# Hybrid diffusion step on one core: row sums beside the out-projection, a last part of three tiles with the prompt tile turned alone, and the first weight sums on VectorE

## The chip, the cores and the metric

The kernel runs on one core of one Trainium2 chip. The metric is the device time of one execution in microseconds (us). The core has five engines with queues of their own: PE (TensorE; its weight loads are listed as PEld), DVE (VectorE), ACT (ScalarE), POOL (GpSimd) and SP (SyncE, which here only issues DMAs). They run side by side and wait for each other by semaphores; each executes its own queue in order. SBUF holds tiles of 128 partitions; PE writes to PSUM.

## What is computed

One layer of a diffusion backbone for 128 prompt tokens and 1024 sample tokens (a 64 x 16 grid), width 1024, float32. Cut to what matters:

```python
def trunk_layer(x, mod, ...):
    shift1, scale1, gate1, shift2, scale2, gate2 = jnp.split(mod, 6, axis=-1)
    h = rmsnorm(x, norm1) * (1 + scale1) + shift1
    mix, new_gla, new_hgrn = hybrid_mixer(h, ...)      # ends with  merged @ w_out
    x = x + gate1 * mix
    h = rmsnorm(x, norm2) * (1 + scale2) + shift2
    x = x + gate2 * conv_ffn(h, w_ffn_up, ffn_conv, b_ffn_conv, w_ffn_down, grid)
    return x, new_gla, new_hgrn

def conv_ffn(h, w_up, conv_w, conv_b, w_down, grid):
    u = dw_conv(h @ w_up, conv_w, conv_b, grid)        # 3x3 over the grid, width 3 for the prompt
    gate, up = jnp.split(u, 2, axis=-1)                # 2816 hidden columns each
    return (jax.nn.silu(gate) * up) @ w_down
```

Both kinds of token go through `trunk_layer` with their own modulation; a last rmsnorm gives `y_prompt` and `y_sample`. The states of the mixer are outputs too and lie ahead of what is changed.

## The kernel before

**Split products.** All large products are made from two parts of each operand: a high part (fp32r, made by ACT as a copy, names ending in `h`) and a low part, the operand less its high part (`split_lo`, line 69, a subtraction on DVE or POOL, names ending in `l`). Each product is three matmuls: high x high, high x low, low x high. So every operand of a product costs one ACT operation and one DVE or POOL operation after it is there.

**Stages.** The mixer runs to about 722 us. Then comes the out-projection `merged @ w_out` with the residual sum, the second norm and its modulation; then the up projection with convolution and gating in 22 chunks of 128 hidden columns (2 x 128 columns of `w_ffn_up` a chunk); then the down projection. The change touches the handover from the mixer to the up projection.

**Out-projection (loop `g` over three groups of three token tiles; lines 1379 and 1392).** Tiles 0 to 7 are sample tokens, tile 8 is the prompt. For groups 0 and 1 most of the product was made beside the mixer and stored; only head block 7 is left. For group 2 (tiles 6, 7, 8) all eight blocks `f` of `w_out` are multiplied here, in the order 1, 2, 0, 3, 4, then 5, 6, 7 tile by tile as the last part, so that the three tiles end one after the other. For each finished tile, `done(i)` multiplies by `gate1` (DVE, L1365), adds x (DVE, L1366) into a tile `x1`, stores it to DRAM (POOL's queue, L1367), makes the reciprocal root of the mean square (`rstd_of`: a Square with a row sum on ACT L377, which writes its squares to `junk`; a small DVE operation L378; a power on POOL L379), and scales into `xn` (ACT, L1370).

**Turning (`modulate2`, line 1314).** PE turns `xn` in 128 x 128 blocks (`transpose`), so that width lies on partitions. For each of eight width blocks `kt` the three tiles of a group go into one PSUM tile; ACT (L1327, odd `kt`) and DVE (L1331, even `kt`) scale and shift it into `RAW[i, j]` (tiles `rb`: i = half of the width, j = half of the sample tokens) and, for tile 8, into `raw_p`.

**Up projection (line 1499).** The sample tokens' product of a chunk is made from seven products of half size in place of eight, in the manner of Strassen: the token operands are b11, b21, b22 and the sums t1 to t4 of `rb` tiles; the weight operands are the four blocks 11, 12, 21, 22 of the chunk and the sums s1 to s4. For a chunk: `load_row` (L1470, SP) loads blocks into `ra`; `weight_sums` (L1490 to 1493, POOL) makes s1 to s4 in `sr`; `split_slots` (ACT L1485, POOL L69) splits into nine slots of the weight tiles `W`. A plan (`plan_slots`) gives the slots of each chunk. The token sums and their splits are made once, on DVE with ACT for the high parts, between lines 1530 and 1562: t1, the prompt (`ph`, `pl`), t2, b22, t3, t4. `queued` writes this order out by hand: each step is put behind the one before on DVE, and on ACT too where it has an ACT part. The sums lie in `tmp[0..3]`, which are the accumulators `acc0..3` of the convolution, not in use yet. The order of the products of the first chunk on PE is 1 (b11), 2 (b21), 5 (t1), prompt, 6 (t2), 3 (b22), prompt, 7 (t3), then the second chunk's 5, then 4 (t4). The prompt's product (L1704) is 12 matmuls in each of two halves, over two weight slots at a time.

**Convolution and gating.** `conv_rows` makes the grid's convolution of a half chunk as one ACT operation (L1628) and eight DVE operations (L1640) that read PSUM. Then Silu (ACT, L1734), the product of the two halves (POOL, L1736), and the store to DRAM (`scr_g`, L1737); `token_sums` makes sums of two chunks for the down projection (POOL, L1593 to 1597).

**Down projection (line 1910).** Again products of half size, 11 pairs of chunks each. Operands are loaded from `scr_g`, `scr_s` and `w_ffn_down` (L128) into raw buffers that are used in turn: quarters of `ra` and `sr`, and two tiles `raw0`, `raw1` of a pool `wh3` on the right side of SBUF, which is opened when the pools of the up projection are closed. ACT makes the high part (L131), DVE or POOL the low part (L69). The pools share SBUF: a tile of a later pool waits until the last reader of the tile that lay there is done.

**What sets the order.** The order of each engine's queue is decided when the program is built, by the framework's planner, which puts operations by estimated times; `issue_after` and `queued` put constraints on it by hand (so do `anchor`'s entries). `next_w` and `prefetch_w` hand out the split weights of the mixer's and the down projection's streams, with loads some slots ahead.

## Time and profile before

| | |
|---|---|
| median of 3 runs | 1573.55 us (1572.3 to 1575.32) |
| the profiled execution | 1575.3 us, of which 1573.2 is the span of the instructions |
| mean granted TensorE clock in it | 0.983 |
| busy: PE, PEld | 1500.9 us (95%), 1258.8 us (80%) |
| busy: DVE, ACT, POOL | 1153.2 us (73%), 788.5 us (50%), 726.3 us (46%) |
| up projection L1499 in the chain that ended last | 26% |
| DMA | 244.61 MB, 155 GB/s mean |

All times within the profile count from the start of the span. A row of the timeline is: start, duration, engine, line, operation, output <- inputs, shape, and how often; in brackets the idle time of the engine just before it and what ended that. "x2" rows cover two instructions from the first start on. A row of the waits is: engine, line and tile that waited <- what released it: us in total, times, longest. A row of the chain of waits is: start, duration, what; it follows the work that ended last back from the end, so that each piece is released by the one above it. A row of the DMA issues gives the median us from issue to landing.

### The profile page before, as it was taken

What the parts mean: (1) busy time and instruction counts of PE and PEld (TensorE: products, weight loads), DVE (VectorE), ACT (ScalarE), POOL (GpSimd) and SP (SyncE); (2) the same over time, 40 slices, a digit from 0 to 9 for tenths busy, and PEclk for the clock granted to TensorE, in tenths of its full rate; (3) what the DMA queues carried; (4) which work ended last, traced back from release to release, by engine and by line L of the source; (5) the groups of instructions that cost most, each with busy time, mean ns of one, the idle gap of its engine ahead of it and who ended that gap; (6) DMA issues with size and microseconds to landing.
All of it is one profiled execution on the core that took longest, in us unless ns stands there. A gap on an engine that the chain in (4) does not pass through costs nothing.

```text
span 1573.2 us, 31068 instructions
## 1 busy us (share of the span) xinstructions
PE 1500.9 (95%) x12506; PEld 1258.8 (80%) x12506; DVE 1153.2 (73%) x1724; ACT 788.5 (50%) x1521; POOL 726.3 (46%) x535
## 2 busy tenths in 40 slices
PE   7999999999999999898879999999999998999997
PEld 2698989998898989676657888888888886788886
DVE  3656566565655768535689999999999999579575
ACT  3565667455454556304564444444444444456444
POOL 1412132234232331102288999999999996000001
PEclk9999999999999999999979999999999999999999
DMA  9311112336434452747411555545644566879762
GB/s 341 113 44 46 46 53 76 96 105 214 113 129 159 133 168 95 297 157 273 158 41 56 169 171 138 131 117 135 197 117 135 176 160 192 321 243 348 248 190 116
DMA packets 164650, 244.61 MB, mean 155 GB/s; under 512 B 11124, under 2 KB 107618, under 8 KB 162586
## 3 DMA queue, kind: packets, MB, share of 16 engines
q1 hardware_dynamic: 142583, 168.54, 33.4%
q0 software_dynamic: 21312, 73.41, 15.2%
q8 instruction: 98, 1.61, 0.4%
q10 hardware_dynamic: 611, 0.68, 0.1%
q14 instruction: 46, 0.38, 0.1%
HBM read 186.95 MB, written 78.71 MB: 169 GB/s over the span
## 4 chain that ended last, share of the span: by engine, by line
PE 82%; DVE 6%; DMA 5%; ACT 3%; issue 3%; POOL 2%; SPq 0%; POOLq 0%; ACTq 0%; DVEq 0%
PE u L1499 26%; PE mm L602 15%; PE xb L1910 7%; PE yb L1910 6%; PE mm L616 5%; PE x L1704 4%; PE mm L745 4%; PE lv L933 3%; PE yb L1961 2%; PE u L1392 2%; PE x L1001 1%; PE mm L505 1%; DMA raw<-in_w_in_dram 1%; DMA wa<-in_w_ada_dram 1%; PE ada L1170 1%
## 5 line engine op out<-in xcount | busy, mean ns | idle before, releaser
L1640 DVE SCALAR_TENSOR_TENSOR acc<-u,convc,acc 128x945 f32<-128x945 f32 (+2 forms) x352 | 427.0, 1218 | 8.3 <-ACT acc L1628 1.7
L69 POOL TENSOR_TENSOR wl<-raw,wh 128x1024 fp32r<-128x1024 f32 x42 | 102.0, 2432 | 247.3 <-ACT wh L131 189.7
L602 PE MATMUL mm<-h1h,wh 128*128 128x384 f32 x528 | 184.9, 350 | 0.7 <-ACT qj L514 0.7
L602 PE MATMUL mm<-h1h,wl 128*128 128x384 f32 x528 | 179.1, 339 | 0.0
L602 PE MATMUL mm<-h1l,wh 128*128 128x384 f32 x528 | 179.1, 339 | 0.0
L896 DVE TENSOR_TENSOR Q<-Q,fb 128x384 f32<-128x384 f32 x126 | 85.9, 682 | 92.6 <-PE lv L933 91.3
L69 POOL TENSOR_TENSOR wul<-sr,wuh 128x512 fp32r<-128x512 f32 (+1 forms) x68 | 123.7, 1820 | 25.8 <-ACT wuh L1485 25.6
L69 POOL TENSOR_TENSOR wul<-ra,wuh 128x1024 fp32r<-128x1024 f32 x46 | 118.9, 2585 | 9.2 <-ACT wuh L1485 6.1
L886 ACT ACTIVATE m<-k 128x384 f32<-128x384 f32 x126 | 70.2, 557 | 83.7 <-DVE k L898 39.4
L1885 POOL TENSOR_TENSOR sq<-sq,mhalf 128x1 f32<-128x1 f32 x9 | 11.1, 1237 | 216.7 <-DVE sq L1882 216.7
L602 PEld LDWEIGHTS mm<-h1h,wh 128*128 128x128 f32 x528 | 99.5, 188 | 5.6 <-issue 3.9
L602 PEld LDWEIGHTS mm<-h1l,wh 128*128 128x128 f32 x528 | 99.5, 188 | 0.6 <-issue 0.2
L602 PEld LDWEIGHTS mm<-h1h,wl 128*128 128x128 f32 x528 | 99.3, 188 | 0.8 <-issue 0.5
L616 PE MATMUL mm<-wh,h1h 128*128 128x256 f32 x288 | 84.4, 293 | 1.3 <-ACT v L641 1.3
L898 DVE TENSOR_TENSOR k<-k,fb 128x384 f32<-128x384 f32 x126 | 74.2, 589 | 12.3 <-ACT m L886 7.2
L131 ACT ACTIVATE wh<-raw 128x1024 fp32r<-128x1024 f32 x55 | 58.2, 1059 | 48.8 <-PE mm L602 11.6
L616 PE MATMUL mm<-wh,h1l 128*128 128x256 f32 x288 | 80.9, 281 | 0.0
L616 PE MATMUL mm<-wl,h1h 128*128 128x256 f32 x288 | 80.9, 281 | 0.0
L1485 ACT ACTIVATE wuh<-ra 128x1024 fp32r<-128x1024 f32 x44 | 46.3, 1053 | 38.0 <-issue 36.1
L1669 ACT ACTIVATE u2p<-u 128x512 f32<-128x512 f32 x44 | 26.3, 597 | 74.4 <-PE u L1499 71.7
L1485 ACT ACTIVATE wuh<-sr 128x512 fp32r<-128x512 f32 (+1 forms) x66 | 50.9, 773 | 22.9 <-PE x L1704 17.0
L1736 POOL TENSOR_TENSOR acc<-acc,acc 128x1152 f32<-128x1152 f32 x22 | 59.1, 2687 | 5.8 <-DVE acc L1640 5.8
(355 smaller groups left out, 4518.6 us busy)
## 6 DMA issues: line engine op xcount, KB each, us to landing
ra<-in_w_ffn_up_dram SPq DMA_DIRECT2D x88, 256.0 KB, 3.1
raw<-in_w_in_dram SPq DMA_DIRECT2D x32, 512.0 KB, 4.6
v<-in_w_ada_dram SPq DMA_DIRECT2D x27, 512.0 KB, 4.4
scr_g<-acc POOLq DMA_DIRECT2D x22, 576.0 KB, 5.5
scr_s<-late POOLq DMA_DIRECT2D x11, 1024.0 KB, 4.6
scr_t<-in_w_ffn_down_dram POOLq DMA_DIRECT2D x16, 704.0 KB, 7.4
wa<-in_w_ada_dram SPq DMA_DIRECT2D x16, 512.0 KB, 6.2
raw<-in_w_out_dram SPq DMA_DIRECT2D x13, 512.0 KB, 3.8
```

The source lines that it names most:

```text
L69: return eng.tensor_tensor(out, full, hi.bitcast(F32), op=ALU.subtract)
L602: anchor["fill"] = mm(ps, a[:, kt, :], h[kt][b], start=(n == 0), stop=(n == 23))
L616: anchor["fill"] = mm(ps, h[kt][t // 3][:, ts_], a[:, kt % 4, :], start=(n == 0), stop=(n == 23))
L745: anchor["fill"] = mm(ps, lhs, ws[f][wi][:, cs], start=(f + n == 0), stop=(f == 6 and n == 2))
L886: nc.scalar.activation(aps(t, 0, [[2 * h, NB], [h, 2], [1, h]]), aps(src, 0, [[2 * h, NB], [BL + h, 2], [1, h]]), AF.Copy)
L896: nc.vector.tensor_tensor(qm, qm, aps(ff_, 2 * h - 1, [[BL - h, 2], [2 * h, NB], [0, h]]), op=ALU.mult)
L898: nc.vector.tensor_tensor(km, km, aps(ff_, BL + 2 * h - 1, [[-(BL + h), 2], [2 * h, NB], [0, h]]), op=ALU.mult)
L1485: nc.scalar.activation(hi, raw, AF.Copy)
L1499: last = mm(dst, W[x][:, a, kt, :], HB[y][b][:, kt, :], start=(start and n == 0), stop=(stop and n == 11), skip_group_check=True,)
L1640: last = nc.vector.scalar_tensor_tensor(o, u3[:, r0 + dy : r1 + dy, c0 + dx : c1 + dx], wc(3 * (dy + 1) + dx + 1), o, op0=ALU.mult, op1=AL ...
L1704: last = mm(pk, HB[h]["p"][:, 4 * half + kt, :], aps(flat(W[x]), a * 512 + kt * P, [[(b - a) * 512, 2], [1, P]]), start=(half + kt + n == ...
L1910: anchor["down"] = mm(banks[i], w[a][:, ts_], w[b][:, 512:1024], start=(start and j == 0 and n == 0), stop=(j == NPAIR - 1 and n == 2), sk ...
```

## The change

1. `done` keeps x1 in the loaded tile `xt` and uses `xn` as the scratch of the Square; the pools `x1` and `junk` are gone, `xn2` has four buffers.
2. The accumulators 0 and 2 are made early, in a pool of their own (`acce`) on the right side of SBUF; 1 and 3 stay on the left. `es_e`, which holds that pool, is closed at the end of the up projection.
3. The weight slots of the out-projection start with `wpb`, and one weight is fetched ahead of the loop over groups (`prefetch_w()`).
4. The order of blocks in group 2 becomes 1, 2, 0, 7, 3, then 4, 5, 6 as the last part. Ahead of block 7, `early_sums()` issues three of the token sums and the first half of t1's split.
5. After group 2, `modulate_last` turns tiles 6 and 7 alone, two width blocks to a PSUM tile; `turn_prompt` turns tile 8 into two PSUM tiles, and `scale_prompt` scales it later, as a step of the queue written by hand.
6. The first chunk's weights: blocks 11 and 12 go to a tile `W0` of their own (low part on POOL); the sums s1 to s4 and the splits of s1, 21/22, s2/s4 and s3 are made on DVE (with ACT) as steps of the hand-written queue, between the token steps. The loads of the second chunk are issued after the 21/22 split. The first chunk's prompt products are 128 columns wide instead of 256, twice as many.
7. The second chunk's weight sums and the split of its s1 come ahead of its 21/22 split. The tile `late` is made after the first chunk's products. t4's splits become steps of the queue, after t3 and the last sums.

```diff
...
-    def rstd_of(sq_pool, x, tag):
...
+    def rstd_of(sq_pool, x, tag, junk=None):
+        if junk is None:
+            junk = sq_pool.tile([P, D], BF16, name="junk", tag="junk" + tag, bufs=1)
...
+    es_e = ExitStack()
+    acce = pool(es_e, "acce", 1, side="right")
+    accs = {i: acce.tile([P, NT], F32, name=f"acc{i}") for i in (0, 2)}
     es_h2 = ExitStack()
     HB = {"h": {}, "l": {}}
     h2a = pool(es_h2, "h2a", 1, side="right")
...
-    xnp2 = pool(es2, "xn2", 3)
-    x1p = pool(es2, "x1", 4)
+    xnp2 = pool(es2, "xn2", 4)
...
+            if g == 0:
+                scaled(kt, 1, RAW[k, 0][:, kk, 0:BL], pt)
+            else:
+                scaled(kt, 1, RAW[k, 0][:, kk, BL:512], pt[:, 0:P])
+                scaled(kt, 1, RAW[k, 1][:, kk, 0:256], pt[:, P:BL])
+
+    def modulate_last(xns):
+
+        for k2 in range(KT // 2):
+            pt = ps_p.tile([P, 2, 256], F32, name="x", tag="x")
+            for h in range(2):
+                for i in range(2):
+                    kt = 2 * k2 + h
+                    nc.tensor.transpose(pt[:, h, i * P : (i + 1) * P], xns[i][:, kt * P : (kt + 1) * P], ident)
+            for h in range(2):
+                kt = 2 * k2 + h
+                scaled(kt, 1, RAW[kt // 4, 1][:, kt % 4, 256:512], pt[:, h, :])
+
+    def turn_prompt(xn):
+
+        got = []
+        for q in range(2):
+            pt = ps_p.tile([P, 4, P], F32, name="x", tag="x")
+            for j in range(4):
+                kt = 4 * q + j
+                nc.tensor.transpose(pt[:, j, :], xn[:, kt * P : (kt + 1) * P], ident)
+            got.append(pt)
+        return got
+
+    def scale_prompt(got):
+        for kt in range(KT):
+            last = scaled(kt, 0, again["p"][:, kt, :], got[kt // 4][:, kt % 4, :])
+            if kt % 2:
+                act = last
+            else:
+                dve = last
+        return act, dve
...
+    def early_sums():
+        for x in "hl":
+            HB[x]["t1"] = h2t.tile([P, 4, 512], F32R, name=f"t1{x}", tag=f"t1{x}")
+        tt(tmp[0], rb(0, 1, 0), rb(0, 0, 0), op=ALU.subtract)
+        tt(tmp[2], rb(1, 1, 0), tmp[0], op=ALU.subtract)
+        split_h("t1", tmp[0], nc.vector, pieces[0])
+        tt(tmp[0], rb(1, 1, 0), rb(0, 1, 0), op=ALU.subtract)
+
+    slots["w"], slots["n"] = [wpb, wpa, wpa, wpa], -1
+    prefetch_w()
     w7 = w_late[7]
     for g in range(3):
...
-            x1 = x1p.tile([P, D], F32, name="x1", tag="x1")
-            nc.vector.tensor_tensor(x1, us[i], gate1[0 if t == 8 else 1], op=ALU.mult)
-            nc.vector.tensor_tensor(x1, x1, xt, op=ALU.add)
-            nc.gpsimd.dma_start(scr_x1[t], x1)
-            st = rstd_of(xnp2, x1, "q")
             xn = xnp2.tile([P, D], F32, name="xn2", tag="xn2")
-            nc.scalar.activation(xn, x1, AF.Copy, scale=st[:, 1:2])
+            nc.vector.tensor_tensor(xn, us[i], gate1[0 if t == 8 else 1], op=ALU.mult)
+            nc.vector.tensor_tensor(xt, xn, xt, op=ALU.add)
+            nc.gpsimd.dma_start(scr_x1[t], xt)
+            st = rstd_of(xnp2, xt, "q", junk=xn)
+            nc.scalar.activation(xn, xt, AF.Copy, scale=st[:, 1:2])
...
-            order = (1, 2, 0, 3, 4, 5, 6, 7)
+            order = (1, 2, 0, 7, 3, 4, 5, 6)
             for fs in [(f,) for f in order[:5]] + [order[5:]]:
-                if fs[-1] == 7:
+                if fs[0] == 7:
+                    early_sums()
+                if fs[-1] == 6:
                     pos["slots"] = 4
                 part = [(f, w_late[f] if f in w_late else next_w(), lhs(f)) for f in fs]
...
-                    if fs[-1] == 7:
+                    if fs[-1] == 6:
                         done(i)
-        modulate2(g, xns)
+        if g < 2:
+            modulate2(g, xns)
+        else:
+            again["p"] = again["late"].tile([P, KT, P], F32, name="raw_p", tag="gate")
+            modulate_last(xns)
+            prompt = turn_prompt(xns[2])
...
-    accs = [accp.tile([P, NT], F32, name=f"acc{i}") for i in range(4)]
+    accs.update({i: accp.tile([P, NT], F32, name=f"acc{i}") for i in (1, 3)})
+    tmp.update({i: accs[i][:, 0:1024].rearrange("p (k n) -> p k n", k=4) for i in (1, 3)})
     p1_t = accp.tile([P, 512], F32, name="cp1")
     h2b = pool(es_h2, "h2b", 1, side="right")
...
+    W0 = again["late"].tile([P, 2, 2, 4, P], F32R, name="w0", tag="mh7")
+    W0 = {x: W0[:, i] for i, x in enumerate("hl")}
+
+    def w_slot(c, nm, x):
+        if c == 0 and nm[0] == "1":
+            return W0[x][:, sorted_by_slot(0, ("11", "12")).index(nm)]
+        return W[x][:, SLOT[c][nm]]
 
...
-    split_slots(0, ("11", "12"), nc.gpsimd)
-    with tc.issue_after(anchor["pow"].ins):
-        weight_sums(0, nc.gpsimd)
-    split_slots(0, ("s1",), nc.gpsimd)
-    split_slots(0, ("s2", "s4"), nc.gpsimd)
-    split_slots(0, ("s3",), nc.gpsimd)
-    split_slots(0, ("21", "22"), nc.gpsimd)
-    load_row(1, 1)
-    load_row(1, 2)
-    tt = nc.vector.tensor_tensor
-    with tc.high_priority():
-        tt(tmp[0], rb(0, 1, 0), rb(0, 0, 0), op=ALU.subtract)
-        tt(tmp[2], rb(1, 1, 0), tmp[0], op=ALU.subtract)
-        split_h("t1", tmp[0], nc.vector, pieces[0])
-        tt(tmp[0], rb(1, 1, 0), rb(0, 1, 0), op=ALU.subtract)
-    order = {"dve": tt(tmp[1], rb(0, 1, 1), rb(0, 0, 1), op=ALU.subtract)}
+    nc.scalar.activation(flat(W0["h"]), flat(ra[:, 0:2]), AF.Copy)
+    split_lo(nc.gpsimd, flat(W0["l"]), flat(ra[:, 0:2]), flat(W0["h"]))
+    order = {"dve": weight_sums(0, nc.vector)}
...
     def split_prompt_tokens():
         first = nc.scalar.activation(HB["h"]["p"], again["p"], AF.Copy)
         return first, split_lo(nc.vector, HB["l"]["p"], again["p"], HB["h"]["p"])
 
-    queued(lambda: split_h("t1", tmp[1], nc.vector, pieces[1]))
+    def q_sum(out, a, b):
+        queued(lambda: tt(out, a, b, op=ALU.subtract))
+
+    def q_split(nm, raw, n):
+        queued(lambda: split_h(nm, raw, nc.vector, pieces[n]))
+
+    def q_slots(*names):
+        queued(lambda: split_slots(0, names, nc.vector, both=True))
+
+    q_slots("s1")
+    q_sum(tmp[1], rb(0, 1, 1), rb(0, 0, 1))
+    q_split("t1", tmp[1], 1)
+    q_slots("21", "22")
+    load_row(1, 1)
+    load_row(1, 2)
+    queued(lambda: scale_prompt(prompt))
     queued(split_prompt_tokens)
-    queued(lambda: split_h("t2", tmp[2], nc.vector, pieces[0]))
-    queued(lambda: tt(tmp[3], rb(1, 1, 1), tmp[1], op=ALU.subtract))
-    queued(lambda: split_h("t2", tmp[3], nc.vector, pieces[1]))
-    parts("b22", [rb(1, 1, n) for n in range(2)])
-    queued(lambda: tt(tmp[1], rb(1, 1, 1), rb(0, 1, 1), op=ALU.subtract))
+    q_split("t2", tmp[2], 0)
+    q_sum(tmp[3], rb(1, 1, 1), tmp[1])
+    q_slots("s2", "s4")
+    q_split("t2", tmp[3], 1)
     for n in range(2):
-        queued(lambda: tt(tmp[2 + n], rb(1, 0, n), tmp[2 + n], op=ALU.subtract))
+        q_split("b22", rb(1, 1, n), n)
+    q_slots("s3")
+    q_sum(tmp[1], rb(1, 1, 1), rb(0, 1, 1))
...
-    parts("t3", tmp[0:2])
-
-    late = again["late"].tile([P, 2304], F32, name="late", tag="mh7")
-    ss_t = late[:, 0:2048].rearrange("p (i n) -> p i n", i=4)
-    pt_t = late[:, 2048:2304]
+    for n in range(2):
+        q_split("t3", tmp[n], n)
+    for n in range(2):
+        q_sum(tmp[2 + n], rb(1, 0, n), tmp[2 + n])
+
...
-                    last = mm(
-                        pk,
-                        HB[h]["p"][:, 4 * half + kt, :],
-                        aps(flat(W[x]), a * 512 + kt * P, [[(b - a) * 512, 2], [1, P]]),
-                        start=(half + kt + n == 0),
-                        stop=(half == 1 and kt == 3 and n == 2),
-                        skip_group_check=True,
-                    )
+                    if c == 0:
+                        names = sorted_by_slot(c, (f"1{half + 1}", f"2{half + 1}"))
+                        outs_in = [(pk[:, j * P : (j + 1) * P], w_slot(c, nm, x)[:, kt, :]) for j, nm in enumerate(names)]
+                    else:
+                        outs_in = [(pk, aps(flat(W[x]), a * 512 + kt * P, [[(b - a) * 512, 2], [1, P]]))]
+                    for j, (o, w) in enumerate(outs_in):
+                        last = mm(
+                            o,
+                            HB[h]["p"][:, 4 * half + kt, :],
+                            w,
+                            start=(half + kt + n + j == 0),
+                            stop=(half == 1 and kt == 3 and n == 2),
+                            skip_group_check=True,
+                        )
...
-            last = split_slots(n, ("21", "22"), nc.gpsimd)
             if n == 1:
-                with tc.issue_after(last.ins):
-                    weight_sums(1, nc.gpsimd)
+                weight_sums(1, nc.gpsimd)
+                split_slots(1, ("s1",), nc.gpsimd)
+            split_slots(n, ("21", "22"), nc.gpsimd)
             if n + 1 < NHID:
                 load_row(n + 1, 2)
...
         if n:
-            split_slots(n, ("s1",), nc.gpsimd)
+            if n > 1:
+                split_slots(n, ("s1",), nc.gpsimd)
             split_slots(n, ("11", "12"), nc.gpsimd)
             if n + 1 < NHID:
...
         if c == 0:
-            with tc.issue_after(last.ins):
-                parts("t4", tmp[2:4])
+            order["dve"] = last
+            for n in range(2):
+                q_split("t4", tmp[2 + n], n)
         up_prompt(c, 1)
+        if c == 0:
+            late = again["late"].tile([P, 2304], F32, name="late", tag="mh7")
+            ss_t = late[:, 0:2048].rearrange("p (i n) -> p i n", i=4)
+            pt_t = late[:, 2048:2304]
         nc.scalar.activation(pt_t, pks[c], AF.Copy)
...
     es_h2.close()
+    es_e.close()
     es3.close()
     es_ps2.close()
...
```

More of the change, by code (lines that the diff above doesn't have):

```diff
@@ L1325, in modulate2 @@
[L1325 to L1333 removed]
+                nc.tensor.transpose(pt[:, i * P : (i + 1) * P], xns[i][:, kt * P : (kt + 1) * P], ident)
@@ L1484, in split_slots @@
             raw = raw.rearrange("p (s n) -> p s n", s=2)
-        nc.scalar.activation(hi, raw, AF.Copy)
-        return split_lo(eng, lo, raw, hi)
+        first = nc.scalar.activation(hi, raw, AF.Copy)
+        last = split_lo(eng, lo, raw, hi)
+        return (first, last) if both else last
     def weight_sums(c, eng):
@@ L1544, in queued @@
             order["dve"] = got
-    def parts(nm, raws):
-        for n, cs in enumerate(pieces):
-            queued(lambda: split_h(nm, raws[n], nc.vector, cs))
     def split_prompt_tokens():
```

64 lines of the change are left out of this document (25 added, 39 removed).

## The prediction

> **What bounds the kernel now.** I read the windows first (busy time of each engine by stage, with the granted TensorE clock), then what PE waited for, then the chain of waits through the handover.
>
> ```profile
> span 1573.2 us, 31068 instructions
> ```
>
> ```profile
> 735.00:781.00 46.00, 43.37 (x196) 33.73 (x196) 26.52 (x35) 27.42 (x38) 6.64 (x9) 0.96 0.62 224
> 781.00:799.00 18.00, 6.78 (x25) 4.46 (x26) 13.92 (x18) 13.12 (x20) 16.15 (x12) 0.65 0.25 91
> ...
> 805.00:823.00 18.00, 13.00 (x68) 10.76 (x66) 16.87 (x9) 10.61 (x13) 11.95 (x6) 0.93 0.10 29
> 823.00:850.00 27.00, 24.87 (x110) 20.06 (x111) 26.50 (x27) 11.47 (x14) 21.65 (x12) 0.92 0.14 39
> ...
> 900.00:1280.00 380.00, 380.00 (x1845) 312.76 (x1845) 366.09 (x386) 174.73 (x234) 364.56 (x243) 1.00 0.53 146
> ```
>
> ```profile
> 1300.00:1330.00 30.00, 23.48 (x93) 17.88 (x92) 28.75 (x28) 10.70 (x13) 17.49 (x9) 0.89 0.64 190
> ...
> 1360.00:1500.00 140.00, 140.00 (x614) 114.94 (x614) 96.30 (x101) 77.06 (x87) 3.81 (x1) 1.00 0.81 277
> ```
>
> After the time stand length, then busy time of PE, PEld, DVE, ACT, POOL. From 900 to 1280 and from 1360 to 1500 PE is busy throughout at clock 1.00: what PE gains or loses before either stretch reaches the end in full. It has holes at two handovers: 781 to 823 (mixer to up projection; DVE is 16.87 of 18 busy there) and 1300 to 1330 (up to down projection).
>
> ```profile
> PE x L1314 <- ACT xn L1370: 9.2, 3, 4.6
> PE u L1499 <- DVE t3l L69: 5.6, 1, 5.6
> ```
>
> ```profile
> 780.76 1.24 DVE x L1365
> ...
> 799.08 1.84 DVE t1l L69
> 801.02 2.27 DVE pl L69
> ...
> 819.09 4.42 DVE t3l L69 x2
> ...
> 824.92 5.39 DVE t4l L69 x2
> 830.32 1.11 DVE acc L1640
> ...
> 841.30 3.06 PE u L1499 x12
> ```
>
> The first handover's end is thus a chain on DVE: x1 and its norm, the operands t1, prompt (pl), t2, b22, t3, t4 in a fixed order, then eight convolution terms, which release PE at 841.30. The last of the operands, t4l, ends at 830.31. I count the handover by that moment. The second one:
>
> ```profile
> PE xb L1910 <- DVE acc L1657: 2.6, 1, 2.6
> PE xb L1910 <- POOL wl L69: 1.7, 1, 1.7
> PE xb L1910 <- ACT wh L131: 1.7, 1, 1.7
> ```
>
> **The change part by part. First handover.**
>
> ```profile
> 734.95 0.61 PE L1314 MATMUL x<-ident,xn 128*128 128x128 f32 x2 [3.41 <-ACT xn L1370]
> ...
> 780.10 0.63 PE L1392 MATMUL u<-wh,mh 128*128 128x512 f32 x2
> ...
> 783.61 1.22 DVE L1530 TENSOR_TENSOR acc<-rb,rb 128x1024 f32<-128x1024 f32 x1
> ...
> 785.23 3.07 POOL L69 TENSOR_TENSOR wul<-ra,wuh 128x1024 fp32r<-128x1024 f32 x1
> ...
> 786.36 3.02 DVE L69 TENSOR_TENSOR t1l<-acc,t1h 128x1024 fp32r<-128x1024 f32 x1 [0.21 <-ACT t1h L1338]
> ...
> 791.54 0.54 DVE L1331 TENSOR_SCALAR rb<-x,s,b 128x256 f32<-128x256 f32 x1 [0.89 <-PE x L1314]
> ...
> 799.80 1.06 ACT L1551 ACTIVATE ph<-raw_p 128x1024 fp32r<-128x1024 f32 x1
> ...
> 823.43 0.69 DVE L1787 TENSOR_TENSOR u<-u,cp 128x512 f32<-128x512 f32 x1
> ```
>
> *Out-projection.* The early split of w_out 0 and the early load of 4 let PE run the products of f=1 inside the 3.41 us before the first transpose; with what else PE does there I take 2.8 of it as won: the last product ends at 777.9 instead of 780.7 (bounds 0 and 3.4). The early sums and t1's first split lie beside PE work and DVE has room for them (26.52 of 46 busy).
>
> *DVE's load.* Out of the path go three early sums at 1.22 and one split that took 3.02: 6.7. Into it come, from POOL, four weight sums and the splits of s1 and s3 at 0.69 (128x512), and those of 21/22 and s2/s4 at 1.22: 6.6. So DVE wins no time by counts. What it can win is waiting: the split at 786.36 took 3.02 instead of 1.22, ending 1.08 after the POOL operation of 785.23 to 788.30. A DVE operation with two SBUF operands and a POOL one exclude each other here, and POOL has fewer of them now.
>
> *To the end of the 21/22 split.* Behind the out-projection DVE's queue holds nine operations of 1024 columns (the remaining gate product, sum and x1 adds, b21l, the t1 parts, the 21/22 split; 11.0), five of 512 (3.5) and four scalings at 0.54 (2.2): 16.7. One POOL turn (the low part of 11/12, some 2.3 left of it) and some 3 us of waiting for the norm of tile 7 and its turning bring it to 777.9 + 22 = 799.9. The norm of that tile is late (its small DVE step stands behind sums in the queue), so products 1 and 2, which don't need it, fill PE meanwhile.
>
> *A new wait.* On ACT, ahead of the prompt's scalings, now stand the high parts of the second chunk's 21/22 and s1. The first needs weights whose load can be issued only once the split just timed has released the buffer.
>
> ```profile
> ra<-in_w_ffn_up_dram SPq DMA_DIRECT2D x88, 256.0 KB, 3.1
> ```
>
> Issue and landing 3.5, so 803.4; the high part 1.06, so 804.5; s1 waits for its POOL sum until 804.8, its high part ends at 805.5. The eight prompt scalings alternate between ACT and DVE until 807.4, ph takes 1.06, pl 1.2: pl ends at 809.6, where it ended at 803.29. Behind the waiting ACT are the scalings and ph; DVE waits for them, PE for DVE.
>
> *From pl to t4l.* DVE has 13 operations at 1.22, one of 0.69 and the two adds at 0.7: 17.9. Before, the same stretch (803.3 to 830.3) was 27.0 long with 12 at 1.22 and the two adds, 16.0, so 11.0 of it were POOL turns and waits. Six POOL operations remain that can cut in; at the 1.1 measured above that is 6.7. Sum 24.6, t4l ends at 834.2: **3.9 us later.** If the new wait doesn't come about, 6.3 go; with all POOL turns gone too it is some 8 earlier than before; with 11.0 for turns it is 8.3 later. Between these I keep 3.9 with -6 to +8. The 24 matmuls more of the first chunk's prompt products cost PE some 2 us, hidden while PE waits for DVE; without that cover, +2.
>
> **Second handover.** Accumulators 0 and 2 move to the right side of SBUF. There, the changed layout puts both where the down phase later has its buffers raw0 and raw1, which before lay over operands that were dead by then.
>
> ```profile
> 1310.23 0.33 SPq L128 DMA_DIRECT2D raw<-scr_g  x1
> ...
> 1312.77 2.29 DVE L69 TENSOR_TENSOR wl<-ra,wh 128x1024 fp32r<-128x1024 f32 x1
> ...
> 1319.25 1.06 ACT L131 ACTIVATE wh<-raw 128x1024 fp32r<-128x1024 f32 x1 [6.58 <-DMA raw<-in_w_ffn_down_dram]
> ...
> 1320.38 4.71 POOL L69 TENSOR_TENSOR wl<-raw,wh 128x1024 fp32r<-128x1024 f32 x2 [6.42 <-ACT wh L131]
> ```
>
> ```profile
> 1324.26 0.63 PE L1910 MATMUL xb<-wh,wl 128*128 128x512 f32 x1
> ...
> 1329.44 0.39 PE L1910 MATMUL xb<-wuh 128*128 128x512 f32 x1
> ```
>
> ```profile
> 1330.33 2.68 POOL L1736 TENSOR_TENSOR acc<-acc,acc 128x1152 f32<-128x1152 f32 x1 [5.23 <-DVE acc L1640]
> ...
> 1333.90 1.34 POOL L1593 TENSOR_TENSOR late<-acc,acc 128x512 f32<-128x512 f32 x1
> ...
> 1335.32 2.17 POOL L1594 TENSOR_TENSOR late<-late,acc 128x512 f32<-128x512 f32 x1
> ...
> 1337.57 2.15 POOL L1596 TENSOR_TENSOR late<-acc,late 128x512 f32<-128x512 f32 x1
> ```
>
> ```profile
> raw<-in_w_ffn_down_dram SPq DMA_DIRECT2D x5, 256.0 KB, 3.2
> ```
>
> The load of raw0, issued at 1310.23, must now wait for the last gate product (POOL, 1330.33 for 2.68), which reads accumulator 0. That product itself comes 2.3 earlier, since the DVE split of 1312.77 now stands behind the convolution: it ends at 1330.7. The load follows; it took 9.0 at 1310.23, and 3.2 is the median there, so it lands between 1334.4 and 1339.8. ACT adds 1.06. POOL does its store issue and three sums first, until about 1337.0, then two low parts of 2.35: the first ends between 1339.4 and 1343.3, the second between 1341.8 and 1345.6. PE has 48 matmuls that need neither buffer (0.23 apart, until about 1324), then waits. At the second low part 68 matmuls of the first product remain: 15.4 at 0.227 apart, and some 2.8 for the slow clock after the wait (before, matmuls were 0.43 apart from 1322.8 to about 1329). So this product ends between 1360.0 and 1363.8. Before, 90 remained at 1329.44: 1349.9. **10 to 14 later, I take 12**; without the clock's loss 7.3.
>
> On that clock the Trainium skill ("TensorE: Matmul & The Clock Gate", Part 1, "What's actually happening") says that some 3.4 us of sustained work release full speed. By it the loss is an estimated 1.6 and the sum 1.2 smaller; in the rows above the slow pace lasted 6 us, and I keep the rows.
>
> SP's queue is in order, so the loads behind raw0 wait too, but their buffers were released at about 1334 to 1340 before as well. All else (the norm's scratch, x1 in the loaded tile, the prompt turned alone) is in the queues counted above.
>
> Sum, against the profiled run's 1575.3 (span 1573.2 and 2.1 around it): 1575.3 + 3.9 + 12 = 1591.2. That run lies 1.75 above the median, 1573.55, so **1589**.
>
> **The rivals.**
>
> 1. *The handover pays, and more than the tail costs.* The prompt's ACT wait doesn't form, the norm comes early, and both waits of PE (9.2 + 5.6) vanish: -14.8; the tail at its least, +7.3: 1573.55 - 7.5 = 1566. For it: those are real PE holes. Against it: DVE is the bound there (16.87 of 18) and its work doesn't shrink. It decides from a handover gain above 7.3. Chance 0.05.
> 2. *The tail is hidden.* If raw0's load were not held back by the gate product, the tail would be as before, and only the handover shows: 1573.55 + 3.9, about 1577 (1571.5 if the wait on ACT is absent too). Against it: accumulator 0 is read by that product, and the buffer lies on it. Chance 0.07.
> 3. *No stall on ACT, tail as worked out.* Handover -6 to 0: 1573.55 - 3 + 12, about 1582. Chance 0.2.
> 4. *Both at their upper bound.* POOL turns as long as before, load in 9.0: +8.3 + 14, 1596. Chance 0.16.
>
> The forecast keeps 0.52, with 1584 to 1594 as its own range.
>
> **How the numbers follow.** About 0.2% (3 us) is what a measurement of this kernel can tell from no change. Faster by more: rival 1 and a corner of 2, 0.06. Within: part of 2, 0.03. Slower: 0.91. The range leaves out rival 1, most of 2 and the end of 4: 1577 to 1598.
>
> **What would show it.** Right: the load of the first raw from scr_g issued some 20 us later than the preceding sr loads, behind POOL's gate product; PE idle for over 10 us around 1328 to 1345, released by ACT wh and POOL wl; DVE idle for some 7 us near 800 while ACT waits for a DMA of ra; t4l's end 4 us later. Each is wrong if its wait isn't there. The forecast falls if PE passes from its first 48 down matmuls to the raw pairs without a wait, or if the operands' chain ends before 827.

## The result and the profile after

The changed kernel takes 1591.88 us (median of 4 runs, 1587.63 to 1594.36); the kernel before took 1573.92 in the same session (4 runs). The ratio is 1.0112 with a 95% interval of 1.0088 to 1.0136: slower, as forecast (1589, range 1577 to 1598).

The windows of the kernel after (columns as in the prediction: start:end, length, busy time of PE, PEld, DVE, ACT, POOL, granted clock, DMA share, GB/s) and its span:

```profile
span 1585.5 us, 31118 instructions
```

```profile
781.00:799.00 18.00, 12.38 (x42) 9.20 (x43) 15.07 (x18) 9.43 (x14) 4.67 (x5) 0.73 0.25 87
799.00:805.00 6.00, 2.91 (x16) 2.25 (x14) 1.34 (x4) 2.46 (x5) 2.83 (x2) 0.95 0.29 87
805.00:823.00 18.00, 15.98 (x74) 14.24 (x75) 16.28 (x13) 12.02 (x15) 8.60 (x5) 0.72 0.10 30
...
900.00:1280.00 380.00, 380.00 (x1842) 312.48 (x1841) 365.95 (x387) 174.30 (x235) 364.50 (x243) 1.00 0.54 148
...
1330.00:1360.00 30.00, 19.74 (x74) 15.46 (x75) 15.97 (x11) 9.14 (x10) 14.55 (x8) 0.74 0.72 246
1360.00:1500.00 140.00, 140.00 (x608) 113.77 (x607) 95.17 (x100) 79.98 (x93) 3.82 (x1) 1.00 0.83 290
```

Two things are new. From 1330 to 1360 PE stands for a third of the time, at clock 0.74. And from 799 to 805 DVE, the engine that bounded the first handover, is busy for 1.34 of 6. The long full stretches are as before.

To add up where the time went, two rows of DVE serve as marks: the last of the mixer's gathering (ev), which stands ahead of everything that the change touches, and t4l. First the kernel before, then after (timeline of DVE: start, duration, engine, line, operation):

```profile
722.57 0.68 DVE L751 TENSOR_TENSOR ev<-ev,v 128x512 f32<-128x512 f32 x1
...
824.83 5.49 DVE L69 TENSOR_TENSOR t4l<-acc,t4h 128x1024 fp32r<-128x1024 f32 x2
```

```profile
720.42 0.68 DVE L752 TENSOR_TENSOR ev<-ev,v 128x512 f32<-128x512 f32 x1
...
806.85 1.23 DVE L69 TENSOR_TENSOR pl<-raw_p,ph 128x1024 fp32r<-128x1024 f32 x1 [1.61 <-ACT ph L1590]
...
826.95 5.32 DVE L69 TENSOR_TENSOR t4l<-acc,t4h 128x1024 fp32r<-128x1024 f32 x2
```

ev ends at 723.25 before and at 721.10 after; t4l ends at 830.32 and 832.27. So the handover, from ev to t4l, grew from 107.07 to 111.17 (**+4.1**), and the rest, from t4l to the end of the span, from 742.88 to 753.23 (**+10.35**). The mixer ahead of ev was 2.15 shorter in this one execution, which is the fastest of the four; that the median is 18 longer and this execution only 12.3 longer comes in part from there. The two stretches make 14.45; where the other 3.5 of the 18 arise, this one profile doesn't show. The end of ev lies anywhere from 718.2 to 728.2 in the profiled executions below, although the kernels hardly differ up to it. The experiments are therefore compared by the two stretches behind ev as well as by their times.

What PE waited for around the second handover of the kernel after (waiter, releaser: us, times, longest):

```profile
PE xb L1977 <- ACT wh L131: 13.2, 1, 13.2
PE xb L1977 <- DVE acc L1712: 1.9, 1, 1.9
PE xb L1977 <- POOL wl L69: 0.8, 1, 0.8
```

The 1.7 behind ACT became 13.2. The timeline there, all engines:

```profile
1330.56 2.61 POOL L1797 TENSOR_TENSOR acc<-acc,acc 128x1152 f32<-128x1152 f32 x1 [13.84 <-DVE acc L1695]
1333.20 0.33 SPq L128 DMA_DIRECT2D raw<-scr_g  x1
...
1338.30 1.06 ACT L131 ACTIVATE wh<-raw 128x1024 fp32r<-128x1024 f32 x1 [13.67 <-DMA raw<-in_w_ffn_down_dram]
...
1339.41 2.07 PE L1977 MATMUL xb<-wh 128*128 128x512 f32 x4 [13.21 <-ACT wh L131]
...
1342.33 0.79 PE L1977 MATMUL xb<-wl,wh 128*128 128x512 f32 x1 [0.85 <-POOL wl L69]
...
1342.83 2.78 POOL L69 TENSOR_TENSOR wl<-raw,wh 128x1024 fp32r<-128x1024 f32 x1
...
1345.48 0.53 PE L1977 MATMUL xb<-wh,wl 128*128 128x512 f32 x1
1345.85 1.09 PE L1977 MATMUL xb<-wh 128*128 128x512 f32 x4
```

The raw load, issued at 1310.23 before, now leaves 0.03 behind the gate product's end (1333.17). Its data are there 5.1 after the issue, then come the high part on ACT and two low parts on POOL, the second ending at 1345.61.

The first handover's new wait, in the chain of waits of the kernel after (start, duration, engine, what, line):

```profile
798.55 3.46 DMA ra<-in_w_ffn_up_dram
802.17 1.27 POOL sr L1544
803.47 0.63 ACT wuh L1538
804.10 0.36 ACT raw_p L1314
805.76 1.06 ACT ph L1590
806.85 0.97 DVE pl L69
...
827.04 5.23 DVE t4l L69 x2
```

The load of ra, then ACT's high parts, the prompt's scalings, ph and pl, in the order that was forecast.

### The profile page after: what moved, and what is told of

Read it like the earlier page. It is cut to its first block, busy times and chain, and to the rows that moved or that the text cites. A ratio compares the mean times of both kernels' runs of the same rounds, so it can differ in the third digit from the quotient of the medians.

```text
span 1585.5 us, 31118 instructions
## 1 busy us (share of the span) xinstructions
PE 1504.5 (95%) x12530; PEld 1263.1 (80%) x12530; DVE 1152.6 (73%) x1732; ACT 788.1 (50%) x1521; POOL 707.8 (45%) x527
## 4 chain that ended last, share of the span: by engine, by line
PE 80%; DVE 6%; DMA 5%; ACT 3%; issue 3%; POOL 2%; SPq 0%; POOLq 0%; ACTq 0%; DVEq 0%
PE u L1553 26%; PE mm L603 14%; PE xb L1977 7%; PE yb L1977 5%; PE mm L617 5%; PE x L1765 4%; PE mm L746 3%; PE lv L934 3%; PE yb L2028 2%; PE u L1441 2%; DMA raw<-in_w_in_dram 2%; PE x L1002 1%; DMA mh<-scr_m 1%; PE mm L506 1%; DVE acc L1695 1%
## 5 line engine op out<-in xcount | busy, mean ns | idle before, releaser
L69 POOL TENSOR_TENSOR wul<-sr,wuh 128x512 fp32r<-128x512 f32 (+1 forms) x65 | 118.5, 1823 | 27.0 <-ACT wuh L1538 26.8
L69 POOL TENSOR_TENSOR wul<-ra,wuh 128x1024 fp32r<-128x1024 f32 x44 | 112.5, 2558 | 4.5 <-ACT wuh L131 3.1
L617 PE MATMUL mm<-wl,h1h 128*128 128x256 f32 x288 | 80.4, 279 | 0.0
```

Source lines behind the costliest of these rows:

```text
L69: return eng.tensor_tensor(out, full, hi.bitcast(F32), op=ALU.subtract)
L617: anchor["fill"] = mm(ps, h[kt][t // 3][:, ts_], a[:, kt % 4, :], start=(n == 0), stop=(n == 23))
```

## The experiments

All times against the kernel before in the same session. The last three columns are the end of ev, the stretch from there to the end of t4l, and from there to the end of the span, all in the profiled execution.

| kernel | median us (runs) | ratio [95%] | ev | to t4l | to the end |
|---|---|---|---|---|---|
| before | 1573.92 (4) | 1 | 723.25 | 107.07 | 742.88 |
| after | 1591.88 (4) | 1.0112 [1.0088, 1.0136] | 721.10 | 111.17 | 753.23 |
| accs_lower | 1581.04 (6) | 1.0047 [1.0029, 1.0065] | 720.94 | 111.51 | 743.25 |
| accs_top_alone | 1586.15 (4) | 1.0083 [1.0064, 1.0102] | 723.85 | 110.38 | 751.57 |
| ph_first | 1593.99 (4) | 1.0133 [1.0113, 1.0153] | 724.20 | 113.42 | 755.28 |
| both | 1583.34 (4) | 1.0068 [1.0049, 1.0087] | 728.23 | 115.17 | 742.10 |
| prompt_first | 1580.26 (4) | 1.0039 [1.0024, 1.0055] | 718.21 | 113.86 | 744.63 |
| sums_on_pool | 1581.99 (4) | 1.0052 [1.0035, 1.0069] | 720.84 | 111.35 | 743.31 |
| prefetch_alone | 1573.75 (10) | 0.9997 [0.9984, 1.0011] | 725.54 | 106.69 | 740.97 |
| before_c1_dve | 1573.79 (10) | 1.0000 [0.9985, 1.0016] | 725.99 | 105.85 | 745.56 |
| before_c01_dve | 1570.36 (10) | 0.9991 [0.9974, 1.0007] | 723.26 | 103.12 | 742.12 |
| lower_c1_dve | 1581.61 (4) | 1.0059 [1.0042, 1.0075] | 721.26 | 111.08 | 744.56 |
| c01_again | 1570.31 (11) | 0.9977 [0.9966, 0.9988] | 722.14 | 103.51 | 742.25 |
| c01_prefetch | 1574.60 (11) | 1.0009 [0.9999, 1.0020] | 723.66 | 104.76 | 744.78 |

### The accumulators' place

Two kernels tell the second handover's cause apart. accs_lower is the changed kernel with accumulators 0 and 2 allocated below the handover's scratch, off the place where raw0 and raw1 later lie:

```diff
-    es_e = ExitStack()
-    acce = pool(es_e, "acce", 1, side="right")
-    accs = {i: acce.tile([P, NT], F32, name=f"acc{i}") for i in (0, 2)}
     es_h2 = ExitStack()
...
     nc.sync.dma_start(modr["B"], scr_mod["B"])
+    es_e, es_h3 = ExitStack(), ExitStack()
+    acce = pool(es_e, "acce", 1, side="right")
+    accs = {i: acce.tile([P, NT], F32, name=f"acc{i}") for i in (0, 2)}
...
-    h2b = pool(es_h2, "h2b", 1, side="right")
+    h2b = pool(es_h3, "h2b", 1, side="right")
```

> The changed kernel, with accumulators 0 and 2 made two pools lower on the right side, so that the down phase's raw0 and raw1 lie again over dead operands; all else as changed. If the late load of raw0 is what the second handover lost: raw0's load is issued at about 1313 instead of 1333, PE waits less than 4 us for ACT wh and POOL wl instead of 14, and the whole falls by some 9.4 to about 1582 (2.7 above before). Rival, the second handover lost to something else (the low part of wl moved behind the convolution, the slow clock): stays at 1588 to 1592.

accs_top_alone is the kernel before with only the accumulators moved up (and x1 kept in the loaded tile, which makes the room):

```diff
+    es_e = ExitStack()
+    acce = pool(es_e, "acce", 1, side="right")
+    accs = {i: acce.tile([P, NT], F32, name=f"acc{i}") for i in (0, 2)}
     es_h2 = ExitStack()
...
-            x1 = x1p.tile([P, D], F32, name="x1", tag="x1")
-            nc.vector.tensor_tensor(x1, us[i], gate1[0 if t == 8 else 1], op=ALU.mult)
-            nc.vector.tensor_tensor(x1, x1, xt, op=ALU.add)
+            nc.vector.tensor_tensor(xn, us[i], gate1[0 if t == 8 else 1], op=ALU.mult)
+            nc.vector.tensor_tensor(xt, xn, xt, op=ALU.add)
```

> The kernel before with parts 1 and 2 of the change alone: x1 kept in the loaded tile, accumulators 0 and 2 at the top of the right side. If the place of the accumulators alone makes the second loss: 9 to 12 above before, 1583 to 1586, with PE waiting some 13 us for ACT wh near 1330, and the first handover as before (last t4l ends at 830 to 831). Rival, the loss needs the new order of the first handover: 1573 to 1575.

The first raw load (timeline of SP's queue) and PE's waits at the second handover, in accs_lower:

```profile
1314.50 0.33 SPq L128 DMA_DIRECT2D raw<-scr_g  x1
```

```profile
PE xb L1977 <- POOL wl L69: 2.4, 2, 1.7
...
PE xb L1977 <- ACT wh L131: 0.8, 1, 0.8
```

and in accs_top_alone:

```profile
1334.69 0.33 SPq L128 DMA_DIRECT2D raw<-scr_g  x1
```

```profile
PE xb L1913 <- ACT wh L131: 10.5, 1, 10.5
```

With the accumulators off that place the load leaves at 1314.50 instead of 1333.20, the wait of 13.2 is 0.8, and the stretch behind t4l is back at 743.25, 0.4 above before. With only the accumulators moved, the wait is there in the kernel before too, and that stretch is 8.7 longer. The place of two tiles causes the loss of the second handover; it is shown from both sides. accs_lower leaves +0.47%, some 7.4 us: its first handover is 4.4 longer than before, and the rest lies in neither stretch of its profile.

accs_top_alone's first handover is 3.3 longer as well, where its expectation had it as before. One row of DVE stands out in it:

```profile
795.67 5.83 DVE L1536 TENSOR_TENSOR acc<-rb,rb 128x1024 f32<-128x1024 f32 x1 [0.38 <-ACT rb L1330]
```

This sum, which takes 1.22 alone, ends only 1.1 after the last of four POOL operations that run without a break from 795.50 to 800.41. Scalings of the prompt stand behind it, and pl begins 82.2 after ev instead of 77.7. So with parts 1 and 2 alone, without any of the new order, the first handover is already longer. What part 1 does in the changed kernel, where accs_lower has it too, was not tested.

### The wait on ACT

ph_first lets ACT do the prompt's ph ahead of the second chunk's high parts; both does so in accs_lower.

```diff
-        first = nc.scalar.activation(HB["h"]["p"], again["p"], AF.Copy)
+        first = anchor["ph"] = nc.scalar.activation(HB["h"]["p"], again["p"], AF.Copy)
...
-                weight_sums(1, nc.gpsimd)
-                split_slots(1, ("s1",), nc.gpsimd)
-            split_slots(n, ("21", "22"), nc.gpsimd)
+            if n == 1: weight_sums(1, nc.gpsimd)
+            with tc.issue_after(anchor["ph"].ins) if n == 1 else nullcontext():
+                if n == 1: split_slots(1, ("s1",), nc.gpsimd)
+                split_slots(n, ("21", "22"), nc.gpsimd)
```

> The changed kernel, with the high parts of the second chunk's s1 and 21/22 on ACT behind the prompt's ph instead of ahead of its scalings; only ACT's and POOL's orders differ, in a few rows. If that wait on ACT is what the first handover lost: ph ends at about 804.5 instead of 806.8, pl and all behind it some 2 earlier, t4l at about 830, the whole 2 lower, 1589 to 1590. Rival, POOL's turns set the chain: pl comes earlier, but t4l still ends at 832 to 833 and the time stays at 1591 to 1592.

> Both edits: accumulators lower and ph first. By the two theories together the changes' losses are gone: 1574 to 1577 (after 1591.9, less 9.4 and 2 to 4). Below 1572 only if the first handover now gains; above 1582 if either theory is wrong.

DVE's scalings of the prompt and a low part further on, first in the kernel after, then in ph_first (timeline; the brackets give the idle time ahead and what ended it):

```profile
801.51 0.85 DVE L1317 TENSOR_SCALAR raw_p<-x,s,b 128x128 f32<-128x128 f32 x2 [3.42 <-PE x L1353]
804.48 0.76 DVE L1317 TENSOR_SCALAR raw_p<-x,s,b 128x128 f32<-128x128 f32 x2 [2.12 <-ACT raw_p L1314]
```

```profile
805.63 1.79 DVE L1317 TENSOR_SCALAR raw_p<-x,s,b 128x128 f32<-128x128 f32 x4 [3.79 <-PE x L1353]
...
809.03 1.23 DVE L69 TENSOR_TENSOR pl<-raw_p,ph 128x1024 fp32r<-128x1024 f32 x1 [1.61 <-ACT ph L1590]
...
814.67 3.38 DVE L69 TENSOR_TENSOR t2l<-acc,t2h 128x1024 fp32r<-128x1024 f32 x1
```

In ph_first DVE no longer waits for ACT between the scalings: all four run in one go. But they begin when PE has turned the prompt, 81.4 after ev (80.4 in the kernel after), because PE does the t1 product first. So pl begins 84.8 after ev instead of 85.7: the wait was worth 0.9, not some 6. And the POOL low parts that ran in the idle stretch now fall among DVE's splits, where a split of 1.22 takes 3.38. The handover came out 2.2 longer than in the kernel after, and both 3.7 longer than accs_lower: no gain on either base. ph_first's time lies above both sides of its expectation, and the time of the kernel named both, 1583.34, on the side where one of the two theories is wrong.

### The prompt's turn on PE, and who does the sums

prompt_first takes both and turns the prompt on PE ahead of the products that follow the second:

```diff
-                nc.tensor.transpose(pt[:, j, :], xn[:, kt * P : (kt + 1) * P], ident)
+                anchor["turned"] = nc.tensor.transpose(pt[:, j, :], xn[:, kt * P : (kt + 1) * P], ident)
...
             for p in (1, 2): up(0, p)
+            anchor["pe"] = anchor["turned"]
```

> The kernel with accumulators lower and ph first, and in it the prompt's eight transposes on PE ahead of the first chunk's t1 product, instead of behind it. Measure: from the end of the mixer's last DVE row (ev) to the end of t4l, 107.1 before, 111.2 after, 115.2 with both edits. If the turn behind the t1 product is what still held the prompt: pl starts some 4 earlier than with both edits, and the stretch falls to 108 to 111; 1577 to 1580. Rival, POOL's turns in the stretch from pl to t4l take it back: pl is earlier, but the stretch stays at 113 or more and the time at 1582 or more.

sums_on_pool is accs_lower with the first chunk's four weight sums back on POOL:

```diff
-    order = {"dve": weight_sums(0, nc.vector)}
+    order = {"dve": weight_sums(0, nc.gpsimd)}
```

> The kernel with accumulators lower, and the first chunk's four weight sums on POOL again instead of DVE; all other steps in their places. If the sums' time on DVE is what delays the stretch between out-projection and prompt: four operations of 0.6 to 0.7 go, ev to t4l falls from 111.5 to about 109, time to 1578. Rival, their POOL turns cost DVE as much as the sums did, and the low part of 11/12 comes later: 111 to 113, time 1581 to 1583.

DVE in prompt_first:

```profile
799.98 2.26 DVE L69 TENSOR_TENSOR pl<-raw_p,ph 128x1024 fp32r<-128x1024 f32 x1 [1.62 <-ACT ph L1590]
...
805.52 3.38 DVE L69 TENSOR_TENSOR wul<-sr,wuh 128x1024 fp32r<-128x1024 f32 x1
```

pl begins 81.8 after ev, 4.0 before the kernel after, so that wait is gone. But from its start to t4l's end it is 32.1 instead of 25.4, with operations of 1.22 at 2.26 and 3.38: the time is handed to POOL's turns. Its whole time, 1580.26, can't be told from accs_lower's (the intervals overlap). The sums' move is neutral: 111.35 against 111.51. By the length of the stretch this is the rival's side of both expectations (prompt_first's time lies between its two sides), and it asks for another account of the handover.

That account counts DVE and POOL as one. From 56 us behind ev to t4l's end, windows of the kernels before and after (the third is below):

```profile
779.25:830.32 51.07, 34.01 (x138) 26.13 (x137) 45.75 (x37) 30.95 (x41) 41.60 (x22) 0.77 0.17 57
```

```profile
777.10:832.27 55.17, 38.65 (x160) 30.61 (x158) 45.76 (x44) 30.28 (x42) 26.52 (x15) 0.81 0.15 48
```

DVE is busy equally long, for more operations; POOL for 15 us less. If the stretches in which at least one of the two runs are added up from their single rows (POOL's issues of DMAs counted, as in the windows), before has 49.7 of 51.1 and after 49.7 of 55.2. The same joint time, and 4.0 more of neither running: that is how the +4.1 divides up. The idle pieces are 3.4 ahead of the first raw_p and smaller ones while the last tile is turned. That these pieces are the cause is argued and not shown. The joint time is not fixed by the work either: added up in the same way, prompt_first, where the piece of 3.4 is 1.5, has 53.3 of 57.9, and accs_top_alone 51.5 of 54.4.

### Fewer turns: POOL's work to DVE

If the two take turns, work should go to whichever does it faster. One row of each kind, on POOL in the kernel before:

```profile
791.73 1.26 POOL L1493 TENSOR_TENSOR sr<-ra 128x512 f32<-128x512 f32 x1
792.96 2.35 POOL L69 TENSOR_TENSOR wul<-ra,wuh 128x1024 fp32r<-128x1024 f32 x1
```

and on DVE in c01_again:

```profile
783.95 0.68 DVE L1493 TENSOR_TENSOR sr<-ra 128x512 f32<-128x512 f32 x1
784.55 1.22 DVE L69 TENSOR_TENSOR wul<-ra,wuh 128x1024 fp32r<-128x1024 f32 x1
```

Three kernels move the sums and low parts of the second chunk (before_c1_dve), of the first two (before_c01_dve), and of the second in accs_lower (lower_c1_dve). before_c01_dve against before:

```diff
-    split_slots(0, ("11", "12"), nc.gpsimd)
+    split_slots(0, ("11", "12"), nc.vector)
     with tc.issue_after(anchor["pow"].ins):
-        weight_sums(0, nc.gpsimd)
+        weight_sums(0, nc.vector)
...
+            we = nc.vector if n == 1 else nc.gpsimd
-            last = split_slots(n, ("21", "22"), nc.gpsimd)
+            last = split_slots(n, ("21", "22"), we)
```

and so for the other slots of these chunks.

> The kernel before, with the second chunk's weight sums and low parts on DVE instead of POOL, nothing else. Theory: through the handover DVE and POOL are one resource, since operations of both with two SBUF operands exclude each other (their union is busy 49.7 of the 51.1 from 56 after ev to the end of t4l before, and 49.7 of 55.2 after); DVE needs 0.6 to 0.7 for 512 columns where POOL needs 1.1 to 1.3, and 1.2 where it needs 2.2 to 2.4. So moving the six to eight POOL operations of that stretch shortens it by 3 to 5: ev to t4l 102 to 104, time 1569 to 1572. Rival: the queue of DVE is the bound and what is added to it adds up, ev to t4l 107 to 112, time 1574 to 1579.

> The same with the first chunk's sums and low parts on DVE as well. One-resource theory: another 5 to 7 less busy, unless DVE's order puts the first product's operands later; ev to t4l 97 to 104, time 1564 to 1572. Rival, DVE's queue is the bound: 110 or more, 1577 or more.

> The changed kernel with accumulators lower, and the second chunk's sums and low parts on DVE. One-resource theory: 3 to 4 less than the 111.5 from ev to t4l, time 1577 to 1578 (1581 with accumulators lower alone). The added waits of DVE for the second chunk's loads, ahead of the prompt's scalings in its queue, work against it. Rival: 112 or more, 1581 or more.

The same window in before_c01_dve:

```profile
779.26:826.38 47.12, 33.20 (x143) 25.34 (x141) 45.69 (x54) 31.44 (x42) 9.95 (x8) 0.82 0.23 78
```

DVE does 54 operations in the time that took 37 before, POOL is nearly empty, and the joint busy time, added up as above, falls from 49.7 to 45.7: the handover is 3.95 shorter. c01_again, the same kernel, has it 3.6 shorter. In lower_c1_dve the joint busy time falls too, from 49.4 to 46.6, but the prompt now comes last:

```profile
PE x L1765 <- ACT ph L1590: 6.3, 1, 6.3
```

and idle time takes it all back (8.5 of 55.1, after 6.1 of 55.5 in accs_lower). before_c1_dve gained 1.2 in the handover (105.85, between the two sides of its expectation, 102 to 104 and 107 to 112) and lost 2.7 behind it; where was not settled. Of the three forecasts made from the joint time, one held, before_c01_dve's.

### The early load alone, and the best version

prefetch_alone takes the out-projection's new part order and early load into the kernel before:

```diff
+    slots["w"], slots["n"] = [wpb, wpa, wpa, wpa], -1
+    prefetch_w()
     for g in range(3):
...
-            order = (1, 2, 0, 3, 4, 5, 6, 7)
+            order = (1, 2, 0, 7, 3, 4, 5, 6)
```

> The kernel before with part 3 and the order of part 4 alone (early split of w_out 0, block 7 fourth), no early sums, weights and prompt as before. If part 3 wins at PE what the after-trace shows (the out-projection ends 56.3 after ev instead of 57.5): the chain behind it, which starts with the last x1 product on DVE, moves with it, ev to t4l 105 to 106, tail unchanged, 1571 to 1573. Rival, the last part with blocks 4, 5, 6 and the loads' new order lose it again: 1574 or more.

No gain that can be measured. The last two kernels are before_c01_dve once more, with 11 runs, and the same with the early load.

> The kernel before with both first chunks' weight sums and low parts on DVE, again, in more rounds: its handover was 3.95 shorter in the profile (103.1 against 107.1), its median 3.7 lower with overlapping spreads. If the shorter stretch reaches the end: 1570 to 1571, ratio to before 0.9975 with an interval below 1. Rival, its median was luck of the mixer's end, which moves by several us from run to run: 1573 to 1575.

> The same with part 3 of the change and its order of blocks (the out-projection ends earlier after ev: 0.4 in the stretch and 1.9 less behind it, where it was tried alone, together within what can be told). Expected 1568 to 1571; no better than the other if the out-projection's end no longer sets what follows.

before_c01_dve had come out at 0.9991 with an interval over 1. Taken again, the same kernel is at 0.9977 [0.9966, 0.9988], some 3.6 us: it beats both kernels by a little, and the two estimates are compatible. The early load on top of it gives 1.0009 where 1568 to 1571 had been expected, its handover 1.3 and its tail 2.5 longer; that loss was not taken apart.

## Why the prediction was right, and which step was wrong

*Second handover: right.* Its cause is shown. Relative to t4l, the gate product began 1.7 earlier than before (forecast 2.3) and the second low part ended 513.3 behind it (forecast 511.5 to 515.3). The load took 5.1, between the bounds of 3.2 and 9.0. The sum of 12 is 1.65 above the measured 10.35. The term for the clock was the one too large: 2.8 behind the second low part. The rows show PE slow from 1339.41 (four matmuls in 2.07), standing for 0.85, and slow again from 1342.33 to about 1345.5, so it was back at full pace when that part came at 1345.61. The forecast took the slow pace to begin with the second low part; it began with the first high part and was over by then. The count erred the other way: 72 matmuls were left and not 68, at 0.227 each 0.9 more. 12 - 2.8 + 0.9 is 10.1, near the measured 10.35.

The Trainium skill ("TensorE: Matmul & The Clock Gate", Part 1, "What's actually happening") gives some 3.4 us of sustained work, and by that rule the sum would have been an estimated 10.8. This trace has 3.2 of slow pace behind the stop of 0.85 and 6.1 from the first slow matmul on, so it doesn't settle that figure.

*First handover: the size right, the reason half wrong.* The forecast had +3.9, measured +4.1.

- Out-projection: 2.8 won was the forecast; its last product ends 56.3 behind ev, by the row below, after 57.5 before (780.73). So 1.2. In prefetch_alone, where that product ends 55.6 behind ev, the time can't be told from before.

```profile
776.80 0.62 PE L1441 MATMUL u<-wh,mh 128*128 128x512 f32 x2
```

- DVE's load by counts unchanged: wrong, and hidden by the waits. Of the three early sums that were to leave the path only one did; two still stand behind the out-projection's last product, which ends at 777.42:

```profile
765.89 1.23 DVE L1383 TENSOR_TENSOR acc<-rb,rb 128x1024 f32<-128x1024 f32 x1 [0.41 <-ACT rb L1314]
...
779.48 1.22 DVE L1384 TENSOR_TENSOR acc<-rb,acc 128x1024 f32<-128x1024 f32 x1
...
786.77 1.21 DVE L1386 TENSOR_TENSOR acc<-rb,rb 128x1024 f32<-128x1024 f32 x1
```

  The count also took the split that does leave at the 3.02 that it lasted beside POOL. At 1.22 each, 2.4 go and 6.6 come, so DVE has some 4 us more of its own work. Its busy time is 45.76 against 45.75 all the same, since that includes its waits for POOL, which runs 15 us less.
- pl ends 6.9 later relative to ev (forecast 6.3): right, and the chain of waits shows the wait on ACT as forecast.
- pl to t4l is 2.8 shorter (forecast 2.4): right.
- "If the new wait doesn't come about, 6.3 go": **this step failed.** ph_first took the wait away and won 0.9 of pl's start, since the scalings then began 81.4 behind ev, when PE had turned the prompt, while the second pair, which had waited for ACT, had begun at 83.4; prompt_first took that away as well and paid in POOL turns what it had won. The step held the wait on ACT for the whole cause, with one price; the runs showed two waits that end within some 2 us of each other, so that taking one away leaves the other, and POOL work that runs beside them without holding DVE up. What grew is time in which neither DVE nor POOL runs, 4.0 of 4.1. That the forecast and the measured size agree so closely is luck in part: the out-projection won 1.6 less than forecast and two sums stayed on the path, and 20.7 instead of 22 from the last product to the end of the 21/22 split made up for most of it. Which part of the change makes the idle time stays open: accs_top_alone, with parts 1 and 2 alone, is 3.3 longer in this handover, by another row. Two slips of the working change nothing: six turns at 1.1 are 6.6 and not 6.7, and with the wait and all turns gone the stretch would have been 9.1 earlier and not some 8.

*The rivals.* "The tail is hidden" fell with the load's issue at 1333.20. "The handover pays" fell with +4.1. "No stall on ACT, tail as worked out" (1582) fell at both ends: the stall came, and without it ph_first was at 1593.99. "Both at their upper bound" did not come about.

*The sum.* +4.1 and +10.35 are 14.45, where 15.9 had been forecast against a profiled execution; the forecast of 1589 is 2.9 below the median. So the median is above the forecast although the two terms came out below it, and the 3.5 us between is in no term of the sum. What the runs leave open is whether an order in which the prompt's pl stands behind t2 would take back the handover's idle time: no kernel tried it.

## To carry to other kernels

When a tile gets a new place, look at what is allocated there next and who reads the old tile last: two tiles moved for the sake of one handover delayed a load at the next, 500 us on, by some 20 us and cost 10.35. Where two engines take turns, count their joint busy time, and the time in which neither runs, before moving work between them; DVE's busy time alone, equal before and after, showed nothing of the 4.1. And before pricing a wait as the cause of a delay, ask what would be late next.

## What was not expected of the hardware

DVE and POOL behave here like one engine over a whole stretch: joint busy 49.7 of 51.1 us before, 49.7 of 55.2 after, with 15 us less on POOL in the second. The Trainium skill ("SBUF — State Buffer", section "SBUF: two separate sides") describes the port pair that they share as an exclusive lock held for a whole instruction. A split of 1.22 that takes 3.38 beside POOL operations agrees with that; the sum of 5.83 in accs_top_alone waited for more than one of them. The surprise is how far it goes: with the work of two chunks moved to the faster engine, 17 operations more on DVE in the same busy time (54 against 37, 45.69 against 45.75) shortened the stretch by 3.95. With one chunk's work moved, the whole time gained nothing (1.0000, and 1.0059 where accs_lower has 1.0047).

The slow pace of PE after waits doesn't follow from the length of the last wait. In the kernel before, waits of 1.66 and 1.72 with two matmuls between them were followed by 6 us of it (in the prediction). In accs_lower, after waits of 0.83 and 1.72, there is none; the next matmuls start 0.23 to 0.34 apart:

```profile
1324.75 0.73 PE L1977 MATMUL xb<-wh 128*128 128x512 f32 x2 [0.83 <-ACT wh L131]
...
1327.20 0.51 PE L1977 MATMUL xb<-wl,wh 128*128 128x512 f32 x1 [1.72 <-POOL wl L69]
1327.54 0.40 PE L1977 MATMUL xb<-wh,wl 128*128 128x512 f32 x1
1327.78 0.40 PE L1977 MATMUL xb<-wl,wh 128*128 128x512 f32 x1
```
